# Attention of a decoder layer in a hand-written TensorE order, with value products in two column halves

## Chip, cores and metric

The kernel runs on one core of a Trainium2 chip. The metric is the device time of one execution in microseconds, the median of three runs. A core has engines that run side by side, each through its own instructions in a fixed order: TensorE (PE, matrix products and transposes, with its weight loads shown apart as PEld), VectorE (DVE), ScalarE (ACT), GpSimd (POOL) and SyncE (SP, which issues DMA transfers here). An engine waits at an instruction until what that instruction needs is there, and everything behind it in its order waits too.

## What is computed

One decoder layer on x of 1024 tokens by 1024 columns, float32. Two head groups stand side by side, dilated attention and an RWKV-7 recurrence; their results are mixed by `w_out`, then comes an FFN:

```python
h = _rms_norm(x, norm_mix_pre[i])
z = h @ w_in
q, k, v = z[..., 0:512], z[..., 512:1024], z[..., 1024:1536]
...
attn = _rms_norm(_dilated_attention(q, k, v), attn_out_gain[i])
rw = _rwkv7(r_r, k_r, v_r, xw, xa, xg, ...)
mixed = jnp.concatenate([attn, rw], axis=-1) @ w_out[i]
x = x + _rms_norm(mixed, norm_mix_post[i])
h = _rms_norm(x, norm_ffn_pre[i])
f = jnp.square(jax.nn.relu(h @ w_ffn_up[i])) @ w_ffn_down[i]
x = x + _rms_norm(f, norm_ffn_post[i])
```

The attention has 8 heads of 64 columns. Each query sees its own past by three patterns (distance up to 128 in steps of 1, up to 512 in steps of 4, up to 2048 in steps of 16); the three results are joined by their softmax denominators. That equals one causal softmax in which a key that is in two or three patterns counts twice or three times.

## The kernel before

**Order in time.** The input projection `z = h @ w_in` runs in slabs (`z_q`, `z_k`, ..., each of 128 columns), with RWKV work of the other engines beside it. Attention's own slabs (`z_aq`, `z_ak`, `z_av`) come last and fill PE while the RWKV chain runs. Each of their results goes to DRAM (`zs_d`, line 683). Up to line 819 the order on PE and SP is written out by a planner (`drive`); what is left of the last slab then is a generator `rest`. Then comes attention (from line 837), the mix by `w_out` and the two FFN parts. From line 1078 on PE's order is again the order of the code. Between these two, in attention, the compiler's scheduler puts each engine's instructions in order by priority and by its own estimate of when operands are there; `high_priority(offset=PRI[3])` lets attention go ahead of the other work, and the other work fills the gaps.

**Attention.** Heads go in four pairs p = 0 to 3, queries in eight tiles i of 128 rows. In `attn_pair(p)`:

- K and Q of each head are read back (`kr`, `qr`, tag "raw", two buffers) and split into a high and a low part in a reduced float format. For Q the two parts lie in the upper and lower 64 partitions of one tile `qs` (POOL, line 844, then DVE, line 845); for K there are two tiles, `kh` (POOL, line 122) and `kl` (DVE, line 854). qs, kh and kl have two buffers each, one for each head of a pair. The order of the loads is qr of head 0 and 1, kr of head 0 and 1, then V (`vT`).
- V is transposed (`vt`, line 863) and copied to `Vt` by ACT (line 864).
- For tile i and head h, the scores of all keys up to the tile's end go to PSUM (`pS`, products with kh and with kl, in pieces of 512 keys). The scores come out negated (Q is scaled by -0.125); DVE adds `strip` (minus the log of how often a key counts, or a large value) and takes the row minimum on the way (line 890), ACT takes the exponential with the row sum (line 893).
- The exponentials are transposed in blocks of 128 keys (`pT`, line 900; two PSUM banks "a" and "c" with one buffer each, for the first four blocks and the rest). ACT copies the first four (line 902), DVE the rest (line 904) to `PT`, four buffers.
- `av` multiplies them with Vt into `po`, one bank for four tiles: for each key block, 128 queries by 64 columns.
- After four tiles, po is divided by the row sums (`rden`, line 910; `ao`, line 912), stored to `a_d`, and its squares summed (`sqa`, line 917; `sq4`, line 918).

PE's instructions, for i and h:

```python
mm(pS[:, :hi - lo], QS[h][:, i * P:(i + 1) * P], (KH, KL)[q][h][:, lo:hi], q == 0, q == 1)
PE.transpose(pt[:, j], Sx[:, (4 * k + j) * P:(4 * k + j + 1) * P], ident)
mm(po[:, ii, h], PTs[h][:, j], Vt[:, j, h * 64:h * 64 + 64], j == 0, j == i)
```

**Work beside it.** In pair 0 the rest of slab `z_av`; then the RWKV half of the mix for three of the eight token tiles: `half_r` loads and transposes it (`mxr`), `half_mm` makes 24 products of 512 columns for a tile (`pm`). The weights of the mix (`WO`, eight tiles) are loaded and split by `load_wo` on ACT and DVE, two after pair 1, two after pair 2, four behind. The third tile's products are put behind the last value product by `issue_after`. Then the attention halves of the mix follow (`half_a` reads a_d back).

Of the kernel before, what the change touches and what calls it, by code (L numbers as in the profile page):

```python
# [40 lines left out]
def hybrid_kernel(tc, x, par, cst, strip, win, wup_lora, gup, gnwb, grow, wout, wup, wdown, out, dbg=None):  # L41
# [4 lines left out]
    def mm(o, lhsT, rhs, start=True, stop=True):  # L46
        return PE.matmul(o, lhsT, rhs, start=start, stop=stop, skip_group_check=True)  # L47

# [5 lines left out]
    with (  # L54
# [780 lines left out]
        last_av = [None]  # L835

        def attn_pair(p):
# [9 lines left out]
            for h in range(2):  # L847
# [12 lines left out]
            for q in range(2):  # L860
                pt = ps.tile([P, 4, P], F32, name=f"vt{p}_{q}", tag="yb"[q], bufs=1)
                for t in range(4):
                    PE.transpose(pt[:, t], vT[:, (4 * q + t) * P:(4 * q + t + 1) * P], ident)
                A.activation(Vt[:, 4 * q:4 * q + 4, :], pt, AF.Copy)
# [4 lines left out]
            def av(po, i, ii, PTs):
                for h in range(2):  # L870
                    for j in range(i + 1):
                        last_av[0] = mm(po[:, ii, h], PTs[h][:, j], Vt[:, j, h * 64:h * 64 + 64], j == 0, j == i)

            for qg in range(2):
                po = ps.tile([P, 4, 2, 64], F32, name=f"po{p}_{qg}", tag="by"[qg], bufs=1)
                for ii in range(4):
                    i = 4 * qg + ii
                    w = P * (i + 1)
                    PTs = []
                    for h in range(2):  # L880
                        Sx = ap_.tile([P, S], F32, name=f"S{p}_{i}_{h}", tag="Sx", bufs=3)
                        mn = sm.tile([P, 2], F32, name=f"mn{p}_{i}_{h}", tag="mn", bufs=4)
                        nbk = 1 if w <= 512 else 2
                        for k in range(nbk):
# [5 lines left out]
                            V.tensor_tensor_reduce(Sx[:, lo:hi], pS[:, :hi - lo], stripT[:, so:so + hi - lo], 1.0,  # L890
                                                   3e38 if k == 0 else mn[:, 0:1], OP.add, OP.min,
                                                   accum_out=mn[:, k:k + 1])
                        A.activation(Sx[:, :w], Sx[:, :w], AF.Exp, scale=-1.0, bias=mn[:, nbk - 1:nbk],  # L893
                                     accum_out=den[:, i, h:h + 1])
                        PT = ap_.tile([P, 8, P], F32, name=f"PT{p}_{i}_{h}", tag="PT", bufs=4)
                        for k in range(nbk):
                            nb_ = min(4, i + 1 - 4 * k)
                            pt = ps.tile([P, 4, P], F32, name=f"pT{p}_{i}_{h}_{k}", tag="ac"[k], bufs=1)
                            for j in range(nb_):
                                PE.transpose(pt[:, j], Sx[:, (4 * k + j) * P:(4 * k + j + 1) * P], ident)  # L900
                            if k == 0:
                                A.activation(PT[:, 0:nb_], pt[:, 0:nb_], AF.Copy)  # L902
# [9 lines left out]
                V.tensor_tensor(ao.rearrange("p t h c -> p (t h) c"), po.rearrange("p t h c -> p (t h) c"),
                                rden[:, 4 * qg:4 * qg + 4].rearrange("p t h -> p (t h)").unsqueeze(2).to_broadcast([P, 8, 64]), OP.mult)
# [531 lines left out]
```

## Time and profile before

| | |
|---|---|
| Runs | 1359.76, 1361.48, 1362.91 us; median 1361.48 |
| Profiled execution | 1361.23 us, of which the span of its instructions is 1359.4 |
| Mean granted TensorE clock | 0.991 of full speed |
| PE | busy 1307.3 us, 96% of the span |
| PEld | 1086.4 us, 80% |
| DVE, ACT, POOL | 67%, 46%, 3% |
| Four head pairs | from 471.5 to 637.5 us of the span |

A row of the groups or of the timeline names the line of the kernel, the engine and the tile that is written and the tiles read; products all stand at line 47, in the helper `mm`, so they are told apart by tile names. A matrix product of 32-bit floats shows as two records. The end of the row, in brackets, is idle time ahead of it and who ended it. In a row of windows, the records of a stretch follow each busy time as (x...).

### The profile page before, as it was taken

To read this page: it belongs to the slowest core of one execution; us is meant where nothing else is said; L and a number is where in the kernel's file an instruction comes from. 1 tells how busy PE (TensorE), PEld (TensorE's weight loads), DVE (VectorE), ACT (ScalarE), POOL (GpSimd) and SP (SyncE) were. 2 spreads that over 40 slices of the span, in tenths; PEclk is the share of its full clock that TensorE was granted. 3 is DMA by queue.
4 is the path that set the end of the run, shared out by engine and by line. 5 is a ranking of instruction groups with operands and counts; after the bars stand their busy time and mean duration, and the time that the engine had idled before them with its cause. 6 is when DMAs were issued, how large, how long until landed. Compare 5 with 4: busy or idle time off the path is not lost.

```text
span 1359.4 us, 22401 instructions
## 1 busy us (share of the span) xinstructions
PE 1307.3 (96%) x8784; PEld 1086.4 (80%) x8784; DVE 914.7 (67%) x1647; ACT 625.0 (46%) x1026; POOL 44.7 (3%) x56
## 2 busy tenths in 40 slices
PE   6999999999999999999998999999999999999997
PEld 5777887788777798988887888888887888888885
DVE  7867658531678567655788986677766786445686
ACT  7652324233555367654656444343434344443442
POOL 0000000000000100110000000000000002000110
PEclk9999999899999999999999999999999999999999
DMA  7346746676685656321434344444366995346564
GB/s 255 114 170 163 194 125 179 184 206 204 182 248 145 194 145 181 102 55 38 138 121 139 132 168 152 168 153 150 132 209 217 322 349 172 95 139 200 186 215 157
DMA packets 161193, 231.02 MB, mean 170 GB/s; under 512 B 51680, under 2 KB 88800, under 8 KB 161088
## 3 DMA queue, kind: packets, MB, share of 16 engines
q1 hardware_dynamic: 153024, 208.62, 48.8%
q10 hardware_dynamic: 8064, 20.98, 4.6%
q8 instruction: 69, 1.13, 0.4%
q14 instruction: 36, 0.29, 0.1%
HBM read 156.66 MB, written 72.89 MB: 169 GB/s over the span
## 4 chain that ended last, share of the span: by engine, by line
PE 77%; DVE 11%; DMA 5%; ACT 4%; issue 2%; SPq 0%; POOL 0%; DVEq 0%; ACTq 0%; POOLq 0%
PE X L47 12%; PE dX L47 9%; PE Z L47 6%; PE pm L47 5%; PE dZ L47 5%; PE po L47 5%; PE dY L47 3%; PE z_av L47 3%; PE z_k L47 3%; PE Y L47 3%; PE pS L47 3%; PE z_v L47 3%; PE z_aq L47 2%; PE pT L900 2%; PE z_r L47 2%
## 5 line engine op out<-in xcount | busy, mean ns | idle before, releaser
L47 PE MATMUL dX<-wow,wou 128*128 128x512 f32 x768 | 176.6, 390 | 3.3 <-ACT wow L1106 1.8
L47 PEld LDWEIGHTS dX<-wow,wou 128*128 128x128 f32 x768 | 143.6, 188 | 35.6 <-DVE wow L1107 3.4
L47 PE MATMUL dZ<-wow,wou 128*128 128x512 f32 x384 | 87.4, 389 | 0.0
L47 PEld LDWEIGHTS dZ<-wow,wou 128*128 128x128 f32 x384 | 72.1, 188 | 14.9
L1106 ACT ACTIVATE wow<-wd 128x1024 fp32r<-128x1024 f32 x40 | 42.3, 1059 | 87.1 <-PE dZ L47 29.8
L1107 DVE TENSOR_TENSOR wou<-ur,wou 128x1024 fp32r<-128x1024 f32 x56 | 72.0, 1288 | 10.8 <-ACT wou L1106 10.5
L47 PEld LDWEIGHTS po<-Vt,PT 128*128 128x128 f32 x576 | 72.6, 191 | 4.8 <-ACT PT L902 2.2
L47 PE MATMUL po<-Vt,PT 128*128 128x64 f32 x576 | 74.0, 269 | 0.7 <-ACT PT L902 0.4
L1107 DVE TENSOR_TENSOR wow<-wd,wow 128x1024 fp32r<-128x1024 f32 x40 | 49.9, 1251 | 36.3 <-ACT wow L1106 35.8
L1106 ACT ACTIVATE wou<-ur 128x1024 fp32r<-128x1024 f32 x56 | 58.6, 1049 | 26.2 <-DMA ur<-u_d 18.8
L893 ACT ACTIVATE S<-S,mn 128x128 f32<-128x128 f32 (+7 forms) x64 | 49.4, 774 | 20.8 <-DVE mn L890 20.7
L890 DVE CUSTOM_DVE_ANT_0 S<-pS,stripT 128x512 f32<-128x512 f32 (+3 forms) x64 | 37.4, 590 | 26.1 <-PE pS L47 15.9
L1193 ACT ACTIVATE r<-u 128x512 f32<-128x512 f32 x48 | 30.1, 627 | 48.4 <-DVE u L1191 48.1
L47 PE MATMUL z_aq<-hT,wh_aq 128*128 128x512 f32 x128 | 47.3, 424 | 3.5 <-DVE ev_v L192 3.5
L47 PE MATMUL pm<-WO,mxr 128*128 128x512 f32 x192 | 48.6, 398 | 0.0
L902 ACT ACTIVATE PT<-pT 128x512 f32<-128x512 f32 (+3 forms) x64 | 32.9, 515 | 32.2 <-PE pT L900 30.2
L1107 DVE TENSOR_TENSOR wow<-TK,wow 128x1024 fp32r<-128x1024 f32 x16 | 20.8, 1301 | 38.9 <-ACT wow L1106 38.9
L47 PE MATMUL Z<-HB,wo 128*128 128x512 f32 x192 | 46.1, 389 | 0.0
L47 PE MATMUL pm<-WO,mxa 128*128 128x512 f32 x192 | 45.8, 394 | 0.0
L900 PE MATMUL pT<-cst,S 128*128 128x128 f32 x288 | 44.4, 276 | 1.0 <-DVE rden L910 0.5
L47 PE MATMUL X<-HB,wo 128*128 128x512 f32 x180 | 43.6, 390 | 1.6 <-ACT HB L1029 1.6
L47 PE MATMUL z_k<-hT,wh_k 128*128 128x512 f32 x128 | 43.2, 398 | 1.7 <-DVE z L223 1.4
(388 smaller groups left out, 3102.5 us busy)
## 6 DMA issues: line engine op xcount, KB each, us to landing
ur<-u_d SPq DMA_DIRECT2D x56, 512.0 KB, 4.2
wd<-in_wdown_dram SPq DMA_DIRECT2D x40, 512.0 KB, 3.9
u_d<-S SPq DMA_DIRECT2D x64, 256.0 KB, 2.1
u_d<-u SPq DMA_DIRECT2D x48, 256.0 KB, 2.1
wr_upa<-in_wup_dram SPq DMA_DIRECT2D x16, 512.0 KB, 3.8
wr_upb<-in_wup_dram SPq DMA_DIRECT2D x16, 512.0 KB, 3.8
TK<-in_wdown_dram SPq DMA_DIRECT2D x16, 512.0 KB, 7.3
x<-in_x_dram SPq DMA_DIRECT2D x8, 512.0 KB, 6.0
```

The source lines that it names most:

```text
L47: return PE.matmul(o, lhsT, rhs, start=start, stop=stop, skip_group_check=True)
L890: V.tensor_tensor_reduce(Sx[:, lo:hi], pS[:, :hi - lo], stripT[:, so:so + hi - lo], 1.0, 3e38 if k == 0 else mn[:, 0:1], OP.add, OP.min, a ...
L893: A.activation(Sx[:, :w], Sx[:, :w], AF.Exp, scale=-1.0, bias=mn[:, nbk - 1:nbk], accum_out=den[:, i, h:h + 1])
L900: PE.transpose(pt[:, j], Sx[:, (4 * k + j) * P:(4 * k + j + 1) * P], ident)
L902: A.activation(PT[:, 0:nb_], pt[:, 0:nb_], AF.Copy)
L1106: A.activation(w[:, 0, 0:n], raw, AF.Copy)
L1107: E.tensor_tensor(w[:, 1, 0:n], raw, w[:, 0, 0:n].bitcast(F32), OP.subtract)
L1193: A.activation(r, src, AF.Relu)
```

## The change

PE's order in attention is now the order of the code, from before the first pair. `attn_pair` is taken apart into `at_load` (Q and K), `at_vt` (V), `at_s` (scores, minimum, exponential of one tile and head), `at_t` (transposes and copies) and `at_v` (values of two tiles, and after four tiles the division and store). A step m is one tile and head, in order of pair, tile, head:

- Scores run two steps (one tile) ahead of transposes. The values of tiles 0 and 1 come after step (2, 1), those of 2 and 3 after (4, 1), those of 4 and 5 at (7, 0), and those of 6 and 7 at (7, 1), behind the first two scores of the next pair. at_load of the next pair stands at (0, 1).
- A value product is split by `mm_h` into two with 64 columns of weights each, into 64 of po's 128 partitions each. `PT` has six buffers in place of four.
- `vt` uses banks "c" and "a" (those of pT) in place of "y" and "b"; pS has bank "z" for its second piece in pair 1 and most of pair 2.
- Of the rest of slab z_av, 28 steps run ahead of attention, one in each of seven steps, and what is left after. load_wo of four weights comes at fixed steps in pairs 0 to 2, the four others in pairs 2 and 3; the RWKV half of the mix for the first two tiles goes in steps of three products (`r_ahead`), from step 45 to 61, and the third behind the last values.

```diff
+    def mm_h(o, lhsT, rhs, start=True, stop=True):
+        for s_ in range(2):
+            last = mm(o[64 * s_:64 * s_ + 64], lhsT[:, 64 * s_:64 * s_ + 64], rhs, start, stop)
+        return last
...
-                pt = ps.tile([P, 4, P], F32, name=f"vt{p}_{q}", tag="yb"[q], bufs=1)
+                pt = ps.tile([P, 4, P], F32, name=f"vt{p}_{q}", tag="ca"[q], bufs=1)
...
-                            pS = ps.tile([P, 512], F32, name=f"pS{p}_{i}_{h}_{k}", tag="w")
+                pS = ps.tile([P, 512], F32, name=f"pS{p}_{i}_{h}_{k}", tag="wz"[k] if p == 1 or p == 2 and i < 6 else "w")
...
-                        PT = ap_.tile([P, 8, P], F32, name=f"PT{p}_{i}_{h}", tag="PT", bufs=4)
+            PT = pts[p, i, h] = ap_.tile([P, 8, P], F32, name=f"PT{p}_{i}_{h}", tag="PT", bufs=6)
...
-                        last_av[0] = mm(po[:, ii, h], PTs[h][:, j], Vt[:, j, h * 64:h * 64 + 64], j == 0, j == i)
+                        mm_h(po[:, i % 4, h], PT[:, j], Vt[:, j, h * 64:h * 64 + 64], j == 0, j == i)
...
-        for p in range(3):
-            with tc.high_priority(offset=PRI[3]):
-                attn_pair(p)
-            if p == 0:
-                for _ in rest:
-                    pass
-            else:
-                load_wo(2 + 2 * p, w2p, "w2")
-                load_wo(3 + 2 * p, w2p, "w2")
...
+        pe_order = tc.manual_schedule(engines={mybir.EngineType.PE})
+        pe_order.__enter__()
...
+        LEAD = 28
+        for _ in range(LEAD):
+            next(rest, None)
...
+        with hi_pri():
+            at_load(0)
+            at_s(*step(0))
+            at_s(*step(1))
+            at_vt(0)
+        for m in range(64):
+            p, i, h = step(m)
+            with hi_pri():
+                if i == 7:
+                    at_t(p, i, h)
+                    if h == 0:
+                        at_v(p, 4)
+                    else:
+                        if p < 3:
+                            at_s(p + 1, 0, 0)
+                            at_s(p + 1, 0, 1)
+                            at_v(p, 6)
+                            at_vt(p + 1)
+                else:
+                    at_s(p, (m % 16 + 2) // 2, h)
+                    at_t(p, i, h)
+                    if h == 1 and i in (2, 4):
+                        at_v(p, i - 2)
+                    if h == 1 and i == 0 and p < 3:
+                        at_load(p + 1)
+            if m < 7:
+                next(rest, None)
+            if m == 7:
+                for _ in rest:
+                    pass
+            if m in (13, 21) or m in (29, 37):
+                k = {13: 4, 21: 5, 29: 6, 37: 7}[m]
+                load_wo(k, w2p, "w2")
+            if m == 31:
+                open_mix()
+            if m in (43, 45, 47, 49):
+                load_wo((m - 43) // 2, M["tp"], "woA")
+            for i_, m0 in ((0, 45), (1, 53)):
+                if m0 <= m < m0 + 9:
+                    next(ahead[i_], None)
...
+        with hi_pri():
+            at_v(3, 6)
+        for _ in ahead[2]:
+            pass
...
-        pe_order = tc.manual_schedule(engines={mybir.EngineType.PE})
-        pe_order.__enter__()
```

The rows below are instructions in an engine's order: line of the kernel, operation, tile written, tiles read, size; names end in tile numbers (pT1_7_0 is pair 1, tile 7, head 0), and x10 means ten in a row.

On PE, at the step from pair 1 to pair 2, before, there were values of tiles 6 and 7 and products of the mix (pm) between the transposes of tile 7 and the first scores of pair 2 (pS2):

```order
L47 MATMUL po1_1_5742<-Vt1_5599,PT1_7_0_5908 128x64 x4
L47 MATMUL pm0_0_6876<-WO4_5984,mxr0_6863 128x512 x3
L47 MATMUL pm0_0_6876<-WO5_5989,mxr0_6863 128x512
L47 MATMUL po1_1_5742<-Vt1_5599,PT1_7_0_5908 128x64 x4
L47 MATMUL pm0_0_6876<-WO5_5989,mxr0_6863 128x512 x2
L47 MATMUL pm0_0_6876<-WO6_6405,mxr0_6863 128x512 x3
L47 MATMUL pm0_0_6876<-WO7_6410,mxr0_6863 128x512
L900 MATMUL pT1_7_1_0_5933<-cst_75,S1_7_1_5921 128x128 x4
L900 MATMUL pT1_7_1_1_5939<-cst_75,S1_7_1_5921 128x128 x4
L47 MATMUL pS2_0_0_0_6038<-kh2_0_6007,qs2_0_5995 128x128
L47 MATMUL po1_1_5742<-Vt1_5599,PT1_7_1_5932 128x64 x4
L47 MATMUL pm0_0_6876<-WO7_6410,mxr0_6863 128x512 x2
```

In PE's order after the change the same place reads:

```order
L47 MATMUL po1_1_6044<-Vt1_5694,PT1_4_0_5870 64x64 x10
L47 MATMUL po1_1_6044<-Vt1_5694,PT1_4_1_5891 64x64 x10
L47 MATMUL po1_1_6044<-Vt1_5694,PT1_5_0_5947 64x64 x12
L47 MATMUL po1_1_6044<-Vt1_5694,PT1_5_1_5969 64x64 x12
L908 MATMUL pT1_7_1_0_6090<-cst_75,S1_7_1_6003 128x128 x4
L908 MATMUL pT1_7_1_1_6096<-cst_75,S1_7_1_6003 128x128 x4
L47 MATMUL pS2_0_0_0_6106<-kh2_0_5744,qs2_0_5732 128x128
L47 MATMUL pS2_0_0_0_6106<-kl2_0_5745,qs2_0_5732 128x128
L47 MATMUL pS2_0_1_0_6113<-kh2_1_5751,qs2_1_5738 128x128
L47 MATMUL pS2_0_1_0_6113<-kl2_1_5752,qs2_1_5738 128x128
L47 MATMUL po1_1_6044<-Vt1_5694,PT1_6_0_5991 64x64 x14
L47 MATMUL po1_1_6044<-Vt1_5694,PT1_6_1_6014 64x64 x14
```

The values of tiles 6 and 7 have moved behind the first scores of pair 2, of both heads, the pm products have left this place, and values of tiles 4 and 5, with 64 columns of weights and in pairs of instructions, stand ahead of the last transposes.

On DVE, at the end of pair 1, before, the copies of transposes (PT) stood between the minima of tile 7 (S1_7), the split of Q of pair 2 (qs2) and that of K (kl2):

```order
L904 COPY PT1_6_0_5850<-pT1_6_0_1_5857 128x384
L890 ISA S1_7_0_5897,mn1_7_0_5898<-pS1_7_0_0_5899,stripT_5030 128x512
L890 ISA S1_7_0_5897,mn1_7_0_5898<-pS1_7_0_1_5903,stripT_5030,mn1_7_0_5898 128x512
L845 SCALAR_TENSOR_TENSOR qs2_0_5995<-qr2_0_5992,qs2_0_5995 64x1024
L904 COPY PT1_6_1_5873<-pT1_6_1_1_5880 128x384
L890 ISA S1_7_1_5921,mn1_7_1_5922<-pS1_7_1_0_5923,stripT_5030 128x512
L845 SCALAR_TENSOR_TENSOR qs2_1_6001<-qr2_1_5998,qs2_1_6001 64x1024
L904 COPY PT1_7_0_5908<-pT1_7_0_1_5915 128x512
L890 ISA S1_7_1_5921,mn1_7_1_5922<-pS1_7_1_1_5927,stripT_5030,mn1_7_1_5922 128x512
L910 RECIPROCAL rden1_5613<-den1_5612 128x8
L854 TENSOR_TENSOR kl2_0_6008<-kr2_0_6004,kh2_0_6007 128x1024
L904 COPY PT1_7_1_5932<-pT1_7_1_1_5939 128x512
```

In DVE's order after the change (rows of 128x1, which only read out a minimum, are left out in both):

```order
L896 ISA S1_7_0_5980,mn1_7_0_5981<-pS1_7_0_0_5982,stripT_5030 128x512
L896 ISA S1_7_0_5980,mn1_7_0_5981<-pS1_7_0_1_5986,stripT_5030,mn1_7_0_5981 128x512
L856 SCALAR_TENSOR_TENSOR qs2_0_5732<-qr2_0_5729,qs2_0_5732 64x1024
L896 ISA S1_7_1_6003,mn1_7_1_6004<-pS1_7_1_0_6005,stripT_5030 128x512
L856 SCALAR_TENSOR_TENSOR qs2_1_5738<-qr2_1_5735,qs2_1_5738 64x1024
L896 ISA S1_7_1_6003,mn1_7_1_6004<-pS1_7_1_1_6009,stripT_5030,mn1_7_1_6004 128x512
L912 COPY PT1_6_0_5991<-pT1_6_0_1_5998 128x384
L912 COPY PT1_6_1_6014<-pT1_6_1_1_6021 128x384
L928 RECIPROCAL rden1_5610<-den1_5609 128x8
L912 COPY PT1_7_0_6031<-pT1_7_0_1_6038 128x512
L865 TENSOR_TENSOR kl2_0_5745<-kr2_0_5741,kh2_0_5744 128x1024
L912 COPY PT1_7_1_6089<-pT1_7_1_1_6096 128x512
```

The copies of tile 6's transposes have moved behind both splits of Q, and kl2_0 keeps its place behind the copy of PT1_7_0.

On PE, in the first tiles of pair 1, before, values (po1_0) of each tile came soon after its transposes:

```order
L47 MATMUL pS1_1_1_0_5651<-kh1_1_5593,qs1_1_5580 128x256
L47 MATMUL pS1_1_1_0_5651<-kl1_1_5594,qs1_1_5580 128x256
L47 MATMUL pS1_2_0_0_5665<-kh1_0_5586,qs1_0_5574 128x384
L47 MATMUL pS1_2_0_0_5665<-kl1_0_5587,qs1_0_5574 128x384
L47 MATMUL po1_0_5614<-Vt1_5599,PT1_0_0_5622 128x64
L900 MATMUL pT1_0_1_0_5634<-cst_75,S1_0_1_5626 128x128
L47 MATMUL pS1_2_1_0_5678<-kh1_1_5593,qs1_1_5580 128x384
L47 MATMUL pS1_2_1_0_5678<-kl1_1_5594,qs1_1_5580 128x384
L900 MATMUL pT1_1_0_0_5645<-cst_75,S1_1_0_5637 128x128 x2
L47 MATMUL po1_0_5614<-Vt1_5599,PT1_0_1_5633 128x64
```

In PE's order after the change:

```order
L47 MATMUL pS1_2_1_0_5769<-kh1_1_5245,qs1_1_5232 128x384
L47 MATMUL pS1_2_1_0_5769<-kl1_1_5246,qs1_1_5232 128x384
L908 MATMUL pT1_1_1_0_5775<-cst_75,S1_1_1_5718 128x128 x2
L47 MATMUL pS1_3_0_0_5781<-kh1_0_5238,qs1_0_5226 128x512
L47 MATMUL pS1_3_0_0_5781<-kl1_0_5239,qs1_0_5226 128x512
L908 MATMUL pT1_2_0_0_5787<-cst_75,S1_2_0_5755 128x128 x3
L47 MATMUL pS1_3_1_0_5794<-kh1_1_5245,qs1_1_5232 128x512
L47 MATMUL pS1_3_1_0_5794<-kl1_1_5246,qs1_1_5232 128x512
L908 MATMUL pT1_2_1_0_5800<-cst_75,S1_2_1_5767 128x128 x3
L47 MATMUL po1_0_5805<-Vt1_5694,PT1_0_0_5714 64x64 x2
L47 MATMUL po1_0_5805<-Vt1_5694,PT1_0_1_5725 64x64 x2
L47 MATMUL po1_0_5805<-Vt1_5694,PT1_1_0_5762 64x64 x4
```

The values of tiles 0 and 1 have moved behind the scores of tile 3 and come in one batch, so that scores and transposes alone stand ahead of them.

More of the change, by code (lines that the diff above doesn't have):

```diff
@@ L921, in hybrid_kernel @@
+            nc.sync.dma_start(a_d[qg * 512:qg * 512 + 512, p * P:(p + 1) * P].rearrange("(t p) c -> p t c", p=P),
+                              ao.rearrange("p t h c -> p t (h c)"))
+            sqa = ap_.tile([P, 4, P], F32, name=f"sqa{p}_{qg}", tag="sqa", bufs=1)
+            A.activation(sqa, ao.rearrange("p t h c -> p t (h c)"), AF.Square)
+            V.tensor_reduce(sq4[:, p, 4 * qg:4 * qg + 4], sqa, axis=AX.X, op=OP.add)
         WO = {}
@@ L1061, in hybrid_kernel, with r_ahead @@
-        pms[2] = pm_new(ORD[2], "zz")
-        with tc.issue_after(last_av[0].ins):
-            half_mm(ORD[2], pms[2], rx.pop(2), 4, True, False)
+        pe_order = tc.manual_schedule(engines={mybir.EngineType.PE})
+        pe_order.__enter__()
+        rx, part, pms = {}, {}, {}
+        def r_ahead(i, keep):
+            rx[i] = half_r(ORD[i], "z")
+            yield
+            pm = pm_new(ORD[i], "zz")
+            for n in range(2):
+                ns = slice(n * 512, n * 512 + 512)
+                for k in range(4):
+                    w = WO[4 + k]
+                    mm3(pm[n], rx[i][:, 0, k], rx[i][:, 1, k], w[:, 0, ns], w[:, 1, ns], k == 0, not keep and k == 3)
+                    yield
+            rx.pop(i)
+            if keep:
+                pms[i] = pm
+                return
+            part[i] = M["mp"].tile([P, D], F32, name=f"y{ORD[i]}", tag="y")
+            for n in range(2):
+                A.activation(part[i][:, n * 512:n * 512 + 512], pm[n], AF.Copy)
@@ new lines, in hybrid_kernel @@
+        ahead = {i: r_ahead(i, i == 2) for i in range(3)}
+        LEAD = 28
+        for _ in range(LEAD):
+            next(rest, None)
+        hi_pri = lambda: tc.high_priority(offset=PRI[3])
+        step = lambda m: (m // 16, m % 16 // 2, m % 2)
+        with hi_pri():
[16 more added lines that the diff above has]
+                            at_vt(p + 1)
+                else:
+                    at_s(p, (m % 16 + 2) // 2, h)
[19 more added lines that the diff above has]
+                    next(ahead[i_], None)
+            if m == 62:
+                for g_ in (0, 1):
+                    for _ in ahead[g_]:
+                        pass
+                next(ahead[2])
```

139 lines of the change are left out of this document (64 added, 75 removed).

## The prediction

> **What bounds the kernel now.** I read the chain of waits first, then the windows of the four head pairs, then the timeline of TensorE (PE). The chain says that PE sets the end:
>
> ```profile
> PE 77%; DVE 11%; DMA 5%; ACT 4%; issue 2%; SPq 0%; POOL 0%; DVEq 0%; ACTq 0%; POOLq 0%
> ```
>
> The change touches only the attention stage. Its windows, one for each head pair, from the pair's first score record to its last value record (us, then busy time and records of PE, PEld, DVE, ACT, POOL; then the granted clock):
>
> ```profile
> 471.50:514.10 42.60, 42.45 (x306) 37.92 (x306) 27.13 (x67) 24.72 (x54) 5.29 (x5) 1.00 0.51 147
> 514.10:556.60 42.50, 40.99 (x307) 36.91 (x306) 31.11 (x75) 28.95 (x62) 4.18 (x4) 1.00 0.63 180
> 556.60:597.60 41.00, 40.99 (x305) 37.19 (x304) 24.96 (x65) 24.04 (x53) 4.57 (x4) 1.00 0.29 71
> 597.60:637.50 39.90, 37.65 (x281) 33.17 (x281) 21.14 (x64) 23.10 (x53) 0.00 (x0) 1.00 0.12 34
> ```
>
> PE has work in 162.1 of 166.0 us, DVE and ACT in 21 to 31 of some 41. So here PE work is time, as long as something is there for PE to do. That condition is what the change puts at risk.
>
> **The values in halves.** A value product is two records of 128x64 weights now (576 records for 288 products); it becomes four records with 64 weight columns each, written alternately to the upper and lower half of the output. The state step of the RWKV part has just this form already (tile O). The timeline, start and length:
>
> ```profile
> 431.66 1.15 PE L47 MATMUL O<-VU,TR 128*64 128x64 f32 x32
> 432.75 0.50 PE L47 MATMUL z_av<-hT,wh_av 128*128 128x512 f32 x1
> 433.08 0.39 PE L47 MATMUL z_av<-hT,wl_av 128*128 128x512 f32 x1
> ...
> 633.77 3.68 PE L47 MATMUL po<-Vt,PT 128*128 128x64 f32 x32
> 637.26 5.71 PE L47 MATMUL pm<-WO,mxr 128*128 128x512 f32 x24
> ```
>
> From start to next start, 32 O records take 1.09 us, 34 ns each, and 32 value records 3.49 us, 109 ns each. So 576 x 0.109 = 62.8 us becomes 1152 x 0.034 = 39.2 us: **23.6 us less PE work**. For this term the trace shows the new form itself, and I take it whole.
>
> The first 512-wide record behind O takes 0.33 us to the next start, against 0.23 us in a run: a switch of form costs 0.1 us. The Trainium skill (TensorEngine Tiling (Array Packing), Key Properties) speaks against the change here: it says that a change of tiling mode drains the array. With 16 batches of values and two switches each, the row's 0.1 us makes that 3.2 us at most, and a full price would be that sum on top; the fine mixture of before had more switches of operation, so I book nothing for it.
>
> **How much PE work is left.** From pair 3's window: 37.65 us, less 8 projection records of 0.23 us each (next row), is 35.8; values of 144 x 0.109 = 15.7 become 288 x 0.034 = 9.8, leaving 29.9; for fewer switches in longer runs I take 28.7 for a pair. Beside it stand the other records that fill PE in this stage, from the chain of waits:
>
> ```profile
> 266.77 9.06 PE z_ak L47 x39
> ...
> 645.78 5.48 PE pm L47 x24
> ```
>
> And the timeline at the first score record:
>
> ```profile
> 471.49 0.33 PE L47 MATMUL pS<-kh,qs 128*128 128x128 f32 x1 [0.40 <-POOL kh L122]
> ```
>
> A 512-wide record takes 0.23 us. Before, the first score record comes at 471.49; by the order rows, 22 more records of the last slab (z_av) now run ahead of it, so attention starts at 471.1 + 22 x 0.23 = 476.1 without a new wait. Still inside are 18 z_av (4.1 us), 48 pm (10.9 us) and 12 transposes for them (1.3 us). Contents: 4 x 28.7 + 4.1 + 10.9 + 1.3 = **131.1 us**. If PE never waited, the last value would end at 607 instead of 637.3. Everything turns on the waits.
>
> **The step from one pair to the next.** K and Q of the next pair go through the buffers of this one. The timeline from the last scores of pair 2 to the first of pair 3:
>
> ```profile
> 585.28 0.40 PE L47 MATMUL pS<-kl,qs 128*128 128x512 f32 x1
> 585.29 1.04 POOL L844 TENSOR_SCALAR qs<-qr 128x1024 fp32r<-128x1024 f32 x1 [31.70 <-PE pS L47]
> ...
> 586.64 1.22 DVE L845 SCALAR_TENSOR_TENSOR qs<-qr,qs 64x1024 fp32r<-64x1024 f32 x1
> ...
> 587.34 1.43 POOL L844 TENSOR_SCALAR qs<-qr 128x1024 fp32r<-128x1024 f32 x1 [1.01 <-PE pS L47]
> ...
> 588.80 1.22 DVE L845 SCALAR_TENSOR_TENSOR qs<-qr,qs 64x1024 fp32r<-64x1024 f32 x1 [0.94 <-POOL qs L844]
> ...
> 594.90 1.04 POOL L122 TENSOR_SCALAR kh<-kr 128x1024 fp32r<-128x1024 f32 x1 [1.17 <-DMA kr<-zs_d]
> ...
> 599.81 1.22 DVE L854 TENSOR_TENSOR kl<-kr,kh 128x1024 fp32r<-128x1024 f32 x1
> ...
> 601.08 0.33 PE L47 MATMUL pS<-kl,qs 128*128 128x128 f32 x1 [0.79 <-DVE kl L854]
> ```
>
> From the last score of head 0 (585.7) to the second head's low part (601.1) it is 15.4 us, and PE waited only 0.79 us at its end, because 19 pm records and values of tiles 4 to 7 lay in between. The change keeps the chain. Loading Q early does not shorten it: qs still needs the old scores done, and kr needs the slot of qr. Stacked in the new DVE order: qs 1.05 + 1.22 behind S half, S half 0.65, second qs 1.22, the kr load 588.80 + 1.22 to 594.90 = 4.9, kh 1.05, kl 1.22 behind a 0.7 copy, small waits: 13.7 us. What PE has in order before that record now: 30 transposes (3.3), one head's scores (1.0), values of tiles 4 and 5 (22 x 0.136 = 3.0), first scores (0.6): 7.9 us. The values of 6 and 7 stand behind the waiting record, and all of PE stands behind it. So 5.8 us of waiting by the stack, 3.8 if kl comes straight after kh and the copies slip behind, 7.5 by the measured 15.4. I take 4.8, between the first two, since DVE has 31 us of work in the fullest of the 42 us windows and room to take kl early. Three such steps, less 1.2 us for a transpose set and three pm records in the last: **13.2 us**, with ends 10 and 21. The DVE rows show a second cause of the same wait: copies of tile 6's transposes stand behind both qs, and the next transposes need that bank.
>
> **The opening of a pair.** Exps of tiles 1 to 5 and copies of tiles 0 to 4, with Vt and sqa (ACT; mean ns; first and last size of each):
>
> ```profile
> L902 ACT ACTIVATE PT<-pT 128x512 f32<-128x512 f32 x40 | 23.8, 594 | 29.2 <-PE pT L900 27.4 <-PE pS L47 1.8
> ...
> L893 ACT ACTIVATE S<-S,mn 128x768 f32<-128x768 f32 x8 | 7.5, 942 | 2.6 <-DVE mn L890 2.6
> ...
> L917 ACT ACTIVATE sqa<-ao 128x512 f32<-128x512 f32 x8 | 5.0, 629 | 10.1 <-DVE ao L912 10.1
> ...
> L929 ACT ACTIVATE WO<-wo,par 128x1024 fp32r<-128x1024 f32 x4 | 4.6, 1145 | 0.2 <-ACT PT L902 0.2
> ...
> L864 ACT ACTIVATE Vt<-vt 128x512 f32<-128x512 f32 x8 | 4.3, 592 | 1.5 <-PE vt L863 1.5
> ...
> L893 ACT ACTIVATE S<-S,mn 128x256 f32<-128x256 f32 x8 | 4.0, 507 | 0.0
> ...
> L902 ACT ACTIVATE PT<-pT 128x128 f32<-128x128 f32 x8 | 2.2, 278 | 1.4 <-PE pT L900 1.4
> ```
>
> Ten exps (0.51 to 0.94, 7.2 in all), ten copies (0.28 to 0.59, 4.7), two Vt and sqa (1.8) make 13.7 us of ACT, near 14.4 with its small waits. PE has 38 transposes (4.2), scores of 10240 columns at 0.23 per 512 (4.6), the values of tiles 0 and 1 (0.8) and some switches: 10.6 us. That is 3.8 us more on ACT. The values of tiles 6 and 7, which could cover it, stand ahead of these scores and not among them; only the copies of tile 0 (0.28 each) and the first Vt (0.59) go beside work of PE that I haven't counted, so 2.6 us of waiting each in pairs 1 and 2, where no filler stands. In pair 0 the filler (4.1 us of projection) covers that, but five WO splits (1.1 each) now stand in ACT's row: 3.0. In pair 3 the pm records cover most: 0.6. Sum **8.8 us**, bounded by 0 (ACT gets ahead during the step from pair to pair) and 16 (3.8 four times).
>
> Smaller: the two banks of pT are single as before, and in tile 5 the second transposes wait for a DVE copy behind three score halves of 0.6: 1.5 us in each of three pairs, but mostly in the same time as ACT's lag above; I book 1.5 once.
>
> **The clock.** Long waits have a second price. The timeline at two waits of the RWKV and FFN stages:
>
> ```profile
> 398.91 1.61 PE L47 MATMUL O<-HV,T 128*64 128x64 f32 x32 [1.55 <-DVE HV L631]
> ...
> 744.28 1.97 PE L1027 MATMUL h2t<-cst,yg 128*128 128x128 f32 x8 [3.07 <-ACT yg L1015]
> 745.89 3.77 PE L47 MATMUL X<-HB,w 128*128 128x512 f32 x12
> 749.50 2.88 PE L47 MATMUL Y<-HB,w 128*128 128x512 f32 x12
> ```
>
> And the windows just behind them, the granted clock third from the end of the row:
>
> ```profile
> 400.00:402.00 2.00, 2.00 (x14) 1.60 (x13) 1.35 (x3) 1.22 (x2) 0.00 (x0) 0.50 0.62 238
> ...
> 743.00:746.00 3.00, 1.72 (x9) 1.73 (x9) 1.80 (x2) 1.22 (x2) 0.00 (x0) 0.69 0.77 238
> 746.00:749.00 3.00, 3.00 (x12) 2.45 (x11) 3.00 (x6) 2.72 (x5) 0.00 (x0) 0.74 0.32 120
> ```
>
> After 3.07 us of waiting the granted clock was 0.69 and 0.74, and 12 records took 3.61 us instead of 2.7: about 1.2 us with the transposes. Behind 1.55 us it was 0.50 for 2 us, which costs 1.0. I book 1.2 for each step between pairs, **3.6 us**; its ends are 0, and 15 with the openings in it (below). The Trainium skill (TensorE: Matmul & The Clock Gate, Part 1) has a rule for it: an idle window of about 3.4 us halves the clock. By that rule alone most waits of this forecast would cost nothing more, and the end would come some 2 us earlier; the trace's 1.55 us stands against it.
>
> **The sum.** 131.1 + 13.2 + 8.8 + 1.5 + 3.6 = 158.2, from 476.1 to 634.3, against 637.3: 3.0 us earlier. What follows (the last 24 pm, the reload of a_d) keeps its order, so it shifts whole. On the profiled execution's 1361.2 us, which is 0.3 below the median of the runs shown, this makes **1358 us**: of the 31 us of work that leave the stretch, 4.6 go ahead of it and 23 come back as waiting and clock.
>
> **Rivals.** *Covered waits (faster):* DVE and ACT are busy in only 53 to 73% of each window, and before the same 15.4 us chain cost 0.79. If value batches overlap with the chain better than my stacking, so that half of the 27.1 us of waits and clock is hidden, the end comes 13 us earlier still: 1345. It decides as soon as kl lands within 10 us of the last scores and ACT enters the opening without a lag. Against it: PE's order is fixed, and no filler is left in pairs 1 and 2. *Low clock (slower):* the short waits of the openings lower the clock as the 1.55 us above did, and it stays at 0.7 through 12 us of work in each of three pairs: 12 / 0.7 - 12 = 5.1 each, 15 us less the 3.6 booked, 1370. It decides once PE's waits come in pieces over 1.5 us every few us. Against it: after 0.79 us at 601 the window of pair 3 has clock 1.00. *The halves don't run side by side*, so that the change doesn't do what it says: at 50 ns a record 18 us come back, of which 52 of 72 value units per pair lie on the path, 13 us: 1371. Against it: 34 ns above.
>
> **How the numbers follow.** My forecast, with its terms part of the way to their ends (1348 to 1368), 0.45; covered waits 0.27; low clock 0.20; halves 0.08. A measurement here tells 0.2%, 2.7 us, from no change. Faster: 0.27 of covered waits and 0.21 of the forecast, 0.48. Same: 0.13 of the forecast, 0.02 of low clock, 0.15. Slower: the rest, 0.37. Range: 1340 leaves out the deepest part of covered waits (0.08), 1375 the worst of the clock and of the halves (0.1). It holds both signs; the forecast's own range stands above.
>
> **What would show it.** Right: po with 1152 records at 34 ns; PE waiting 3 to 6 us before pS of pairs 1 to 3 for kl or for DVE; ACT as releaser of pT in openings; PE busy near 131 of 158 us. Wrong: PE gaps under 2 us at those steps and an end of the last value before 625 (covered waits), or after 642 with a clock below 0.9 in a pair's window (low clock); O-like records above 40 ns.

## The result: 0.5% slower

Six runs of each kernel: median 1368.95 us (1365.94 to 1370.77) after the change, 1362.2 us (1359.76 to 1364.3) before; ratio **1.005**, 95% interval 1.0032 to 1.0067. The forecast was 1358, faster. The profiled execution took 1369.49 us with a span of 1367.7, against 1361.23 and 1359.4. Of all runs below, one (1416.96 us, of order_alone_filled) counts as slow and is left out of its median and ratio.

The windows of the four head pairs in the profile after, from each pair's first score to the next pair's (the last one to the end of the last value), answer to the four of before:

```profile
479.00:518.00 39.00, 32.90 (x316) 26.55 (x314) 29.00 (x68) 27.31 (x57) 5.27 (x4) 0.91 0.67 215
518.00:559.00 41.00, 31.36 (x421) 26.21 (x419) 25.71 (x69) 23.63 (x55) 4.68 (x4) 0.96 0.29 85
559.00:599.30 40.30, 33.05 (x423) 27.08 (x423) 24.39 (x66) 22.74 (x51) 4.30 (x4) 0.96 0.30 86
599.30:645.70 46.40, 44.61 (x588) 39.14 (x588) 22.47 (x65) 27.14 (x58) 0.00 (x0) 0.96 0.10 30
```

PE now has work in 141.9 of 166.7 us and stands still in the rest, and the granted clock, 1.00 in all four windows before, is 0.91 to 0.96. What PE waited for in this stretch, summed (us in total, times, longest; the first five rows of eight, which make 23.9 us):

```profile
PE pT L908 <- DVE PT L912: 12.2, 7, 3.9
PE pT L908 <- ACT Vt L878: 2.9, 4, 1.0
PE pS L47 <- DVE kl L865: 2.8, 2, 1.8
PE pT L908 <- ACT PT L910: 2.4, 5, 0.8
PE pS L47 <- DVE mn L896: 2.2, 4, 0.8
```

The largest is not the wait for kl that the prediction put first, but transposes that wait for DVE's copies: 9.7 of the 12.2 us stand in the three steps between pairs, at the copy of tile 6's transposes, the second cause that it named; the other 2.5 stand at the transposes of tile 5. DVE's timeline in the step from pair 0 to pair 1 shows why:

```profile
505.62 1.22 DVE L856 SCALAR_TENSOR_TENSOR qs<-qr,qs 64x1024 fp32r<-64x1024 f32 x1
506.87 0.69 DVE L896 CUSTOM_DVE_ANT_0 S<-pS,stripT 128x512 f32<-128x512 f32 x1
...
507.78 1.22 DVE L856 SCALAR_TENSOR_TENSOR qs<-qr,qs 64x1024 fp32r<-64x1024 f32 x1 [0.21 <-POOL qs L855]
509.03 0.75 DVE L896 CUSTOM_DVE_ANT_0 S<-pS,stripT,mn 128x512 f32<-128x512 f32 x1
...
509.71 0.55 DVE L912 COPY PT<-pT 128x384 f32<-128x384 f32 x1
```

And PE's, at the same place:

```profile
506.21 0.60 PE L908 MATMUL pT<-cst,S 128*128 128x128 f32 x4
510.41 2.68 PE L908 MATMUL pT<-cst,S 128*128 128x128 f32 x11 [3.60 <-DVE PT L912]
513.02 4.14 PE L47 MATMUL po<-Vt,PT 128*64 128x64 f32 x88
```

The copy that frees bank "c" stands on DVE behind both splits of Q; PE waits 3.60 us for it. Behind the wait, 11 transposes take 2.61 us to the next start and 88 value records 4.07, 46 ns each, where 88 take 2.72 (31 ns each) in pair 3. The windows there show the granted clock (third from the end):

```profile
509.00:512.00 3.00, 1.59 (x8) 1.38 (x8) 2.97 (x8) 1.24 (x2) 0.61 (x1) 0.54 0.90 244
512.00:515.00 3.00, 3.00 (x42) 2.67 (x42) 3.00 (x4) 0.59 (x1) 1.78 (x2) 0.50 0.63 202
515.00:518.00 3.00, 3.00 (x65) 2.93 (x63) 1.46 (x2) 0.22 (x2) 0.54 (x1) 0.83 0.77 265
...
560.00:563.00 3.00, 3.00 (x71) 3.00 (x66) 0.00 (x0) 0.39 (x2) 0.00 (x0) 0.57 0.66 180
```

Where the time went can be summed from the timeline: for each PE record the time to the next record's start, less the idle time noted there, by the tile that it writes (us).

| | before | after | halves_alone (below) |
|---|---|---|---|
| stretch | 471.4 to 637.3 | 479.0 to 645.7 | 471.8 to 639.2 |
| values (po), groups in a row | 60.4 in 80 | 40.7 in 16 | 47.5 in 78 |
| transposes (pT) | 29.7 | 35.2 | 33.6 |
| scores (pS) | 43.7 | 44.7 | 49.4 |
| z_av | 10.9 | 4.7 | 10.8 |
| pm, mxtr, vt | 17.7 | 17.5 | 18.4 |
| waits | 3.5 | 23.9 | 7.6 |

The values give 19.7 us; waits take 20.4 and slower transposes 5.5, in part through the clock. Of the 8.3 us between the two profiles, 2.9 lie ahead of attention, in code that the change doesn't touch: the last z_aq record starts at 458.24 before and 461.12 after, and in the profiles of this study it lies between 458 and 463. So below I also give the time from that record's start to the end of the last value, 179.0 us before and 184.5 after, which leaves this out.

### The profile page after: what moved, and what is told of

Its sections match the earlier page's. It is cut to its first block, busy times and chain, and to the rows that moved or that the text cites. A ratio compares the mean times of both kernels' runs of the same rounds, so it can differ in the third digit from the quotient of the medians.

```text
span 1367.7 us, 23518 instructions
## 1 busy us (share of the span) xinstructions
PE 1291.0 (94%) x9360; PEld 1063.5 (78%) x9360; DVE 914.4 (67%) x1647; ACT 626.3 (46%) x1026; POOL 45.9 (3%) x56
## 4 chain that ended last, share of the span: by engine, by line
PE 74%; DVE 13%; DMA 6%; ACT 4%; issue 2%; SPq 0%; POOL 0%; DVEq 0%; ACTq 0%; POOLq 0%
PE X L47 11%; PE dX L47 8%; PE Z L47 6%; PE pm L47 6%; PE dZ L47 5%; PE z_aq L47 3%; PE dY L47 3%; PE z_av L47 3%; PE po L47 3%; PE z_ak L47 3%; PE Y L47 3%; PE z_v L47 3%; PE z_k L47 3%; PE pT L908 2%; PE pS L47 2%
## 5 line engine op out<-in xcount | busy, mean ns | idle before, releaser
L1178 ACT ACTIVATE wou<-ur 128x1024 fp32r<-128x1024 f32 x56 | 58.5, 1048 | 20.9 <-DMA ur<-u_d 13.4
L908 PE MATMUL pT<-cst,S 128*128 128x128 f32 x288 | 47.1, 290 | 18.4 <-DVE PT L912 12.2
L898 ACT ACTIVATE S<-S,mn 128x128 f32<-128x128 f32 (+7 forms) x64 | 49.4, 772 | 19.2 <-DVE mn L896 18.4
L908 PEld LDWEIGHTS pT<-cst,S 128*128 128x128 f32 x288 | 34.4, 146 | 28.7 <-issue 11.1
L896 DVE CUSTOM_DVE_ANT_0 S<-pS,stripT 128x512 f32<-128x512 f32 (+3 forms) x64 | 37.6, 590 | 23.5 <-PE pS L47 18.6
L47 PE MATMUL pm<-WO,mxr 128*128 128x512 f32 x192 | 49.4, 400 | 0.5 <-DVE mxr L972 0.5
L47 PE MATMUL X<-HB,wo 128*128 128x512 f32 x180 | 43.6, 390 | 1.6 <-ACT HB L1034 1.6
L47 PE MATMUL z_av<-hT,wh_av 128*128 128x512 f32 x128 | 44.9, 405 | 0.0
```

The source lines that it names most:

```text
L1178: A.activation(w[:, 0, 0:n], raw, AF.Copy)
```

## The experiments

All ratios are to the kernel before on the same chip, with their 95% intervals; the last column is the time from z_aq to the end of the last value in the profile.

| kernel | median us | ratio | us |
|---|---|---|---|
| before | | 1 | 179.0 |
| after | 1368.95 | 1.005 (1.0032 to 1.0067) | 184.5 |
| halves_alone | 1365.1 | 1.0004 (0.9981 to 1.0026) | 180.0 |
| order_alone | 1416.27 | 1.0392 (1.0351 to 1.0433) | 229.5 |
| av4_early | 1370.52 | 1.0049 (1.0029 to 1.007) | 183.3 |
| av6_ahead | 1365.23 | 1.0014 (0.9993 to 1.0035) | 182.5 |
| both_moves | 1360.1 | 0.9971 (0.9952 to 0.999) | 174.9 |
| both_and_act_copy | 1355.39 | 0.994 (0.9917 to 0.9963) | 176.1 |
| filled_waits | 1365.72 | 1.0005 (0.9985 to 1.0025) | 179.2 |
| order_alone_filled | 1400.35 | 1.0263 (1.0204 to 1.0321) | 227.2 |
| third_buffer | 1366.04 | 1.0011 (0.9988 to 1.0034) | 181.0 |
| best_vt_bank | 1354.21 | 0.9928 (0.991 to 0.9947) | 173.0 |

### One half of the change at a time

The kernel of before with the halves, and the kernel after without them:

```diff
 halves_alone (on before)
-                        last_av[0] = mm(po[:, ii, h], PTs[h][:, j], ...
+                        last_av[0] = mm_h(po[:, ii, h], PTs[h][:, j], ...
 order_alone (on after)
-                        mm_h(po[:, i % 4, h], PT[:, j], ...
+                        mm(po[:, i % 4, h], PT[:, j], ...
```

> The kernel of before, with only the value products split in two column halves; order left to the scheduler, PT with four buffers. Theory A (PE work is what counts as long as something is in its order to do, and the hand order gives the gain of the halves back as waits for DVE at the step between pairs): PE was busy in 162 of 166 us of attention, the halves take 23.6 us out, DVE and ACT have 21 to 31 us in each window of then 36: 15 to 20 us faster than before, ratio 0.985 to 0.989. Rival B (without that PE work the chain of scores, exponentials and transposes over DVE and ACT sets the pace in any order): at most 6 us faster, ratio 0.995 or more. Records of po 31 to 36 ns apart by both.

> The kernel after the change, but value products whole (128 columns of weights), as before. Theory A: 23.6 us of PE work come back; of it the batches of tiles 4 and 5 stand before the wait for kl at the step between pairs and fill some of it, the rest is on the path: 17 to 22 us slower than after, that is ratio 1.017 to 1.021 to the kernel before. Rival B (engines other than PE set the pace): 8 us slower than after or less, ratio to before below 1.012.

Halves alone change nothing (ratio 1.0004): outside theory A's range, and within B's, but not for B's reason. PE didn't stand still, it lost the gain beside the values. Three rows of before, in PE's timeline of pair 0:

```profile
484.29 0.62 PE L900 MATMUL pT<-cst,S 128*128 128x128 f32 x4
484.75 0.78 PE L47 MATMUL po<-Vt,PT 128*128 128x64 f32 x6
485.34 0.47 PE L47 MATMUL pS<-kh,qs 128*128 128x512 f32 x1
```

The same place in halves_alone:

```profile
488.73 0.60 PE L906 MATMUL pT<-cst,S 128*128 128x128 f32 x4
489.25 0.57 PE L47 MATMUL po<-Vt,PT 128*64 128x64 f32 x12
489.75 0.33 PE L47 MATMUL pS<-kh,qs 128*128 128x128 f32 x1
```

Six whole records take 0.59 us from start to start. Twelve halved ones take 0.50, not the 0.37 of their 31 ns, and the four transposes ahead of them 0.52 instead of 0.46. In the table above, values cost 47.5 us instead of 1152 x 0.031 = 35.7, and scores and transposes 5.7 and 3.9 more: 21.4 us over 78 groups, 0.27 a group, **0.14 us for each switch** between the forms. The rest of the gain went into waits (7.6 us, 3.5 before), most of it for the load of vT (4.5).

The order alone costs 3.9%, where the theories allowed 2.1% at most. By the same sum its values take 78.1 us, 37 more than in after, since PE runs at half clock for long stretches; two windows (the clock third from the end), and the value batch in them from the timeline:

```profile
516.00:522.00 6.00, 6.00 (x30) 6.00 (x29) 3.29 (x3) 0.60 (x1) 2.19 (x2) 0.50 0.67 221
522.00:528.00 6.00, 6.00 (x30) 6.00 (x30) 0.07 (x1) 0.60 (x1) 0.00 (x0) 0.50 0.12 51
```

```profile
516.70 9.49 PE L47 MATMUL po<-Vt,PT 128*128 128x64 f32 x44
```

44 whole value records take 9.28 us, 211 ns each instead of 109. PE is never idle in these 12 us, and the clock doesn't come back. One step later, behind a wait of 3.88 us, it does, with the same batch of 44 whole records running (it starts at 576.77):

```profile
574.00:577.00 3.00, 2.66 (x13) 2.50 (x14) 0.86 (x3) 1.06 (x2) 1.04 (x1) 0.54 0.67 175
577.00:580.00 3.00, 3.00 (x26) 3.00 (x25) 1.53 (x2) 0.60 (x1) 1.04 (x1) 0.89 0.00 0
580.00:583.00 3.00, 3.00 (x29) 3.00 (x29) 0.29 (x1) 0.29 (x1) 0.00 (x0) 1.00 0.53 171
```

What made the difference isn't shown. So neither half gains by itself, and they need each other: the halves pay only in long groups, which the order makes, and the order alone costs far more than with the halves.

### The price of a switch by itself

48 value products are added to the kernel after, in whole form (more_switches, whose edit is shown) or in halves (more_halves, with mm_h in place of mm), each overwritten by the group behind it:

```diff
+                    if (i, h) != (i0, 0):
+                        mm(po[:, i % 4, h], PT[:, 0], Vt[:, 0, h * 64:h * 64 + 64], True, True)
```

> The kernel after the change, with 48 added value products in the whole form (128 columns of weights), one ahead of each head's and tile's group in the batches but the first; each is overwritten by the group behind it, so the output is the same. They add 96 records and 96 switches between whole and halved columns. Theory S (a switch between the forms costs about 0.12 us, as the profile of halves_alone has it): records at 0.105 us and switches make 10 + 11.5 = 21 us of PE time in attention, seen as the time from start to start of the value records; those in the batches of tiles 4 to 7 lie partly in waits. Rival (a switch is free): 10 us of it.

> The control of more_switches: the same 48 added products, but in column halves, 192 records, no switch of form added. By both theories 192 x 0.034 = 6.5 us of PE time more than after; so more_switches minus this is 15 us by theory S and 3.5 us by its rival.

The groups by form, first two rows of more_switches, then one of more_halves:

```profile
L47 PE MATMUL po<-Vt,PT 128*64 128x64 f32 x1152 | 48.3, 229 | 0.0
L47 PE MATMUL po<-Vt,PT 128*128 128x64 f32 x96 | 20.9, 299 | 0.0
```

```profile
L47 PE MATMUL po<-Vt,PT 128*64 128x64 f32 x1344 | 44.8, 229 | 0.0
```

Summed from start to start, values take 61.3 us with the switches and 43.6 without: 17.7 more, where theory S had 15 and its rival 3.5. Of it 96 x 0.104 - 192 x 0.032 = 3.8 are the records, so 13.9 us for 96 switches, again 0.14 each. The clock differed a little between the two runs; a batch at full clock in both, first in more_switches, then in more_halves, shows the same:

```profile
628.53 2.46 PE L47 MATMUL po<-Vt,PT 128*64 128x64 f32 x30
617.87 1.27 PE L47 MATMUL po<-Vt,PT 128*64 128x64 f32 x36
```

To the next start they take 2.39 and 1.20 us: 1.19 more for six whole records in place of twelve halves, and for six switches. By the same figures for the records that is 0.16 a switch. The one run of each took 1388.61 and 1374.16 us. The Trainium skill (TensorEngine Tiling (Array Packing), Key Properties) says that a change of tiling mode drains the array; the runs agree that such a change costs time, and give the price, but don't show that it is a drain.

### The step between pairs

```diff
 av4_early: values of tiles 4 and 5 ahead of the transposes of tile 6, head 1
-                    if h == 0:
-                        at_v(p, 4)
...
+                    if i == 6 and h == 1:
+                        at_v(p, 4)
                     at_t(p, i, h)
 av6_ahead: values of tiles 6 and 7 ahead of the next scores
+                            at_v(p, 6)
                             at_s(p + 1, 0, 0)
                             at_s(p + 1, 0, 1)
-                            at_v(p, 6)
```

> The kernel after the change, with one move in PE's order: the values of tiles 4 and 5 stand ahead of the transposes of tile 6, head 1, not behind those of tile 7, head 0. Nothing else is edited. In the profile of after, PE stood 3.6 and 3.85 us at those transposes for a DVE copy behind both splits of Q, the clock was 0.50 to 0.57 for some 5 us behind it, and the copy of PT7_0 on DVE waited 2.1 us for just these values (six buffers), with kl behind it. Theory A1 (place of the wait and DVE's queue): the wait is filled by 3 us of values, the clock stays at 1, kl lands 1 to 2 us earlier: 3 to 4 us for each of three steps, 8 to 12 us faster than after, ratio to before 0.996 to 0.999. Rival A2 (the chain from the old scores through qs, kr, kh to kl, 14.4 us, sets the step whatever PE does in it): the wait moves to pS and kl, 0 to 3 us faster than after, ratio 1.003 to 1.005.

> The kernel after the change, with one move in PE's order: the values of tiles 6 and 7 stand ahead of the first two scores of the next pair, not behind them. Theory A2 (the chain sets the step): 4 us of values come into the 14.4 us of the chain, in place of behind it; what PE waits for there (3.6 to 7 us a step) is filled: 8 to 12 us faster than after, ratio 0.996 to 0.999. Theory A1 (the wait is the DVE copy that holds bank c, ahead of this place): the values don't fill it, kl was waited for by 1.8 and 1.5 us in two steps only; at most 4 us faster, and the first scores of the pair come later: ratio 1.002 to 1.006.

Neither theory covers both results. av4_early halves the waits for DVE's copy, 12.2 to 6.2 us, and gains nothing: PE waits at kh, kl and the copies of ACT in their place, as A2 said. av6_ahead brings 0.4%, less than A2 said; kl isn't waited for any more, but the 3.6 us at the copy stand. Two limits lie in the same step, so I put both moves in one kernel, and in a second one let ACT make the late copy:

```diff
+                elif i == 6 and p < 3:
+                    A.activation(PT[:, 4:4 + nb_], pt[:, 0:nb_], AF.Copy)
                 else:
                     V.tensor_copy(PT[:, 4:4 + nb_], pt[:, 0:nb_])
```

> The kernel after the change with both moves in PE's order together: values of tiles 4 and 5 ahead of the transposes of tile 6, head 1, and values of tiles 6 and 7 ahead of the first scores of the next pair. Theory C (two limits lie one behind the other in the step between pairs, the DVE copy that holds bank c and the chain of 14.4 us over qs, kr, kh to kl; either move alone meets the other limit): some 12 us of PE work now lie inside the chain, the wait of a step falls from 6.5 us (with its clock) to 2 to 3 us: 9 to 12 us faster than after, ratio to before 0.996 to 0.998. Rival D (what comes early there is lost again in the opening, where ACT is behind): at most 3 us better than av6_ahead alone, ratio 0.999 to 1.002.

> As both_moves, and the second copies of tile 6's transposes (bank c) are made by ACT in pairs 0 to 2 in place of DVE, so that they don't stand behind the splits of Q. Theory C: the rest of the wait at bank c goes, kl on DVE comes 0.5 to 1 us earlier a step: 1 to 4 us faster than both_moves, ratio to before 0.993 to 0.997. Rival D: no difference from both_moves beyond 0.001.

Both moves together bring 0.8% (1.005 to 0.9971) where each alone brought 0 and 0.4%, and with the ACT copy 0.994, as theory C had it. From after to both_moves, waits fall from 23.9 to 17.5 us, and the clock lost (summed as below) from 7.4 to 3.1. The ACT copy's own share is less sure: its interval overlaps that of both_moves, and while waits for DVE's copies fall from 6.1 to 2.5 us, those for ACT's rise from 3.8 to 6.6. (The profile of the latter has a wait of 3.3 us for the first load of vT, so that its time in the last column is too long by that.) From the start of head 0's last score to the start of the second head's low part, the steps take 14.8, 15.2 and 13.8 us after the change and 16.7, 15.6 and 13.5 with both moves; but there the values of tiles 6 and 7, 3.7 us, lie inside the step, and after the change they follow it.

### The clock

14 products of 512 columns, whose results nobody uses, fill the wait at the copy in pairs 0 and 1:

```diff
+                    if i == 6 and h == 1 and p < 2:
+                        dm = ps.tile([P, 512], F32, name=f"dm{p}", tag="b", bufs=1)
+                        for _ in range(14):
+                            mm(dm, at[p][1][1][:, :P], at[p][1][1][:, :512])
                     at_t(p, i, h)
```

> The kernel after the change, with 14 added products of 512 columns (results unused, K of the same pair) ahead of the transposes of tile 6, head 1, in pairs 0 and 1: they need nothing that is late and take 3.2 us of the 3.6 and 3.85 us that PE waited there. Theory K (PE standing still is what lowers the clock): granted clock 0.95 to 1 in the 6 us behind, where after had 0.50 to 0.57; the 11 transposes and the values of tiles 4 and 5 take 1.3 + 2.8 us and not 2.7 + 4.1; PE comes to the next pair's scores up to 2.7 us earlier and waits for kl there: 0 to 3 us faster than after, ratio to before 1.002 to 1.005. Rival L (the batches of transposes and values lower the clock themselves): clock 0.5 to 0.6 there as before, ratio 1.005 to 1.007.

> The same 14 products in order_alone (hand order, whole value products), whose PE ran at a granted clock of 0.50 from 514 to 548 us and from 588 to 597 us, each after a wait at this place or at kl. Theory K: without the wait the clock stays near 1 in step 0 to 1 at least: 15 to 30 us faster than order_alone, ratio to before 1.017 to 1.029. Rival L (whole value products in long batches hold the clock down by themselves): ratio 1.036 to 1.042.

PE's timeline in filled_waits, in the step from pair 0 to pair 1:

```profile
507.69 3.38 PE L47 MATMUL dm<-kh 128*128 128x512 f32 x14
510.91 0.60 PE L908 MATMUL pT<-cst,S 128*128 128x128 f32 x4
511.91 0.52 PE L908 MATMUL pT<-cst,S 128*128 128x128 f32 x3 [0.40 <-DVE PT L912]
...
514.21 2.79 PE L47 MATMUL po<-Vt,PT 128*64 128x64 f32 x88
```

And the windows there:

```profile
509.00:512.00 3.00, 2.60 (x15) 1.98 (x14) 2.75 (x7) 0.59 (x1) 0.25 (x1) 1.00 0.79 195
512.00:515.00 3.00, 2.24 (x37) 1.84 (x39) 3.00 (x4) 1.14 (x3) 1.05 (x1) 1.00 0.78 216
515.00:518.00 3.00, 3.00 (x80) 2.93 (x75) 2.66 (x4) 0.98 (x2) 1.93 (x1) 1.00 0.55 165
```

With the wait filled, the clock stays at 1.00, and 88 value records take 2.72 us to the next start, not 4.07. PE does 6.4 us of useless work, and the kernel is 0.45% faster than after: 1.0005, intervals apart, even better than theory K's range, since the two steps themselves shrank from 14.8 and 15.2 to 13.4 and 12.6 us. (I had held them for fixed. The likely reason, not tried by itself: DVE's copies and kl behind them wait for PE's slow transposes and values.) In order_alone the same filling brings 1.3% of 3.9%; the clock falls there to 0.50 again behind later waits, one of 1.84 us for kl among them. So theory K holds where the wait was filled; what is left open is what else holds the clock down in order_alone, long batches of whole values among it.

### Two more for a faster kernel

third_buffer adds a buffer for the loads and takes one from PT; best_vt_bank moves half of V's transposes from bank "a" to "b". Both stand on both_and_act_copy:

```diff
 third_buffer
-tag="raw")
+tag="raw", bufs=3)
-tag="PT", bufs=6)
+tag="PT", bufs=5)
 best_vt_bank
-tag="ca"[q]
+tag="cb"[q]
```

> As both_and_act_copy, with three buffers for the loads of Q, K and V in place of two, and five for PT in place of six (there is room for no more): the load of K's first head no longer waits for the split of Q. Theory C (the chain over the loads still counts): kl 3 to 5 us earlier, V earlier by as much, so that PE waits less for the first scores and for vT: 2 to 5 us faster than both_and_act_copy, ratio to before 0.990 to 0.993. Rival: kl isn't waited for any more there, what is left are the openings and the copies: within 0.001 of both_and_act_copy, 0.993 to 0.995.

> As both_and_act_copy, with the second half of V's transposes in bank b (free until the first values of the pair) in place of bank a, for which the first transposes of the pair waited 1.0 to 1.5 us in three of four openings (2.9 us in all) until ACT had copied Vt. If PE's order sets the openings: those waits go, 2 to 3 us faster than both_and_act_copy, ratio to before 0.991 to 0.993. Rival (ACT is what the openings wait for, as I priced them): the same time is waited for a few instructions later, at the copies of pT: ratio 0.993 to 0.995.

third_buffer fell outside both theories: slower than both_and_act_copy, 1.0011. Its waits and a stretch of DVE's timeline:

```profile
PE pS L47 <- DVE mn L896: 9.3, 5, 4.1
PE pT L908 <- ACT PT L910: 8.1, 11, 2.3
```

```profile
511.70 2.05 DVE L865 TENSOR_TENSOR kl<-kr,kh 128x1024 fp32r<-128x1024 f32 x1
513.78 1.22 DVE L856 SCALAR_TENSOR_TENSOR qs<-qr,qs 64x1024 fp32r<-64x1024 f32 x1
515.03 0.69 DVE L896 CUSTOM_DVE_ANT_0 S<-pS,stripT 128x512 f32<-128x512 f32 x1
```

K was there early, so the scheduler put its split (kl) ahead of the minima of tile 7 on DVE, and PE waited for those minima (9.3 us, 2.2 in both_and_act_copy): a shorter chain, at a worse place in DVE's order. Whether the five PT buffers cost something too wasn't tried.

best_vt_bank is the fastest kernel of the study, 1354.21 us, 0.7% faster than before. Its waits on PE begin:

```profile
PE pT L908 <- ACT PT L910: 8.8, 15, 1.9
PE pT L908 <- DVE PT L914: 2.5, 3, 1.5
```

The 2.9 us for Vt are gone, but waits for ACT's copies grew from 6.6 to 8.8 us: mostly the rival, with ACT as what the openings wait for. Its 0.9928 and the 0.994 of both_and_act_copy lie within each other's intervals, so this last edit isn't shown to help.

## Why the prediction was wrong

The forecast had the end of the last value at 634.3; the profile has 645.7. Term by term:

- **Values, 23.6 us: right.** In both_moves, at nearly full clock, they take 36.7 us instead of 60.4, 23.7 less (both some 2.4 below the forecast's 39.2 and 62.8). In after the clock takes 4 of it back.
- **Start of attention, 476.1: right.** 479.02, of which 2.9 lie ahead of the change's reach.
- **Contents, 131.1: the step that failed first.** PE worked 142.8 us. Windows of 3 us over the whole stretch, busy time times what the clock lacks, give 7.4 us of lost clock, so 135.4 at full clock, 4.3 above the forecast. By what PE works on, at full clock: values 36.7 us (39.2 forecast), the projection and mix rows 18.8 (16.3), scores, transposes and vt 79.9 (75.6). The last is where the sum failed: "for fewer switches in longer runs I take 28.7 for a pair" was a discount of 1.2 a pair on 29.9, taken from no row, and without it 80.4 us would have stood there, and 135.9 in all. Before had switches of operation but not of form. At 0.14 us the new ones cost 4.5 us (16 batches with two each, an estimate from the two experiments above); the row that the prediction quoted (0.33 instead of 0.23 us behind O) showed such a price, and it booked nothing for it. So whatever the longer runs saved, switches and the like took about as much; how the two share the 79.9 isn't shown.
- **Clock, 3.6: mis-sized by a factor of two.** 7.4 us. The 1.2 us a step came from one wait in the FFN stage; here the clock was 0.50 to 0.57 for 3 to 6 us behind the wait, and in the step from pair 1 to 2 it fell twice.
- **Waits, 23.5: the sum was right (23.9), partly by luck.** The steps between pairs took 13.1 us (13.2 forecast): 3.60 from pair 0 to 1, 3.85 and 1.84 from 1 to 2, four small ones of 3.8 in the last. The wait stood mostly at bank "c" (9.7 us); with that place filled in av4_early, PE waits for kh, kl and ACT's copies instead. Openings took 5.4 (8.8 forecast), and what is left 5.4 (1.5 forecast), DVE's copies in tile 5 with 2.5 and minima with 2.2 among it: two errors that cancel.

4.3 of contents, 3.8 of clock, 0.4 of waits and 2.9 of start make the 11.4 us between forecast and profile. With the first two the sum would have said some 1366, slower.

Of the rivals, low clock (1370) came nearest to the measured time, by luck: it had 15 us of lost clock behind the waits of the openings. In after those, 1.0 us and less, left the clock at 1.00 (in both_moves one of 1.45 us did lower it); the waits of the steps lowered it, by 7.4 us in all. Its sign was half met: the last value ended after 642, but no pair's window had a clock below 0.9. Covered waits and halves not side by side both fell: PE waited as long as booked, and at full clock the records of a batch do run 30 to 35 ns apart.

## What to carry to other kernels

A narrower form of matrix product that is faster in a long run can lose everything in a fine mixture: count the switches of form, and price each from a row that shows one. Where two waits lie in one dependent step, taking one away shows little (here 0 and 0.4%, against 0.8% for both); move work into the step as a whole, ahead of whichever instruction waits. And a wait on PE can cost more than its length: behind 3.60 us of it, 88 records took 4.07 us instead of 2.72. So look there first for a place to put batches that keep PE fed.

## What the runs showed of the hardware

In after, the granted clock fell to 0.50 behind the wait of 3.60 us (window 512 to 515), to 0.57 behind one of 1.84 us (560 to 563) and to 0.54 behind two of 0.60 and 0.93 us close together (602 to 605); behind one of 1.51 us by itself it stayed at 1.00 (542 to 548). In both_moves it fell to 0.74 and 0.69 behind one of 1.45 us (526.3 to 532.3), so the length of a wait alone doesn't settle it. It came back within 3 to 6 us behind halved values, scores and transposes, but in order_alone it stayed at 0.50 through 12 us of unbroken work, nearly all of it whole value records: a busy PE is not always enough to get it back. The kind of record alone doesn't decide it, since from 577 us on it came back with the same records running. The Trainium skill (TensorE: Matmul & The Clock Gate, Part 1) has the clock back after about 3.4 us of sustained work; the return from 577 us on, behind a wait that ended at 574.34, agrees with that, and the 12 us from 516 on don't.
